# Source order on three engines in a Strassen-Winograd up-projection, rotating staging places and respaced norm steps

## The chip, the cores and the metric

The kernel runs on one core of a Trainium2 chip. The metric is device time of one execution in microseconds. Engines: PE is TensorE (matmul; PEld its weight loads), DVE is VectorE, ACT is ScalarE, POOL is GpSimd, SP is SyncE, which only issues DMAs here.

## The reference

One inference step of a two-layer decoder trunk with width 1024: 1024 prompt tokens and eight decode tokens, which the kernel carries as 1032 columns. Layer 1 is an HGRN2 recurrence, layer 2 a sliding-window attention, each beside a cross-attention into 256 memory tokens. Both end in an output projection and a squared-ReLU MLP of width 4096:

```python
mix = jnp.concatenate([tok_out, x_out], axis=-1) @ w_out[l]
h = h + rms_norm(mix, norm_post_mix[l])
u = jnp.square(jax.nn.relu(rms_norm(h, norm_pre_mlp[l]) @ w_up[l]))
h = h + rms_norm(u @ w_down[l], norm_post_mlp[l])
```

Outputs are the hidden states, the memory keys and values, the recurrent state and the last 128 keys and values.

## The kernel before

Everything is f32. A product is made of three matmuls (`mm3`, lines 287 to 289): operands are split into a high part (a cast on ScalarE, line 225) and a low part (a subtraction on GpSimd, line 98), and low x high, high x low and high x high are summed in PSUM. VectorE's instructions all pass through the wrapper `InOrder` and therefore show as line 51.

`mlp` is run once per layer. Its up-projection has 32 output tiles of 128 rows. Six are plain dense tiles. The other 26 are taken as 13 pairs, and `pair` computes a pair by the seven block products of a Strassen-Winograd scheme, which the code names 11, 22, S2, 12, S3, S1 and S4. Each product is 24 matmuls of 128x258 (two column halves c = 0 and 1, four blocks, three matmuls), so a pair is 168 matmuls. Products accumulate into PSUM banks: 11 and 12 into `ac` (two banks), 22 and S1, S4 into `ax` (four), S2 and then S3 into the same two `dn` banks. So S3 can't start in a half before VectorE has added that half's S2 result into `u2` (the rows `k<-k,dn`).

For the next pair, `load_blocks` has ScalarE issue four weight DMAs (`wr<-wu`), `sum_blocks` forms S1 to S4 of the weights on VectorE (four operations of 128x512), and `split_block` splits the seven blocks one by one into a ring of ten places (ScalarE cast, GpSimd subtraction).

A pair's last part, `last()`, is put behind the next pair's first product (`pending`): it splits the hidden block B21 into the tile `mv` (`split_21`) and stores it with one DMA (`u21s<-mv`), runs product S4, forms three hidden differences on VectorE and one on GpSimd (`hidden_sums`, 128x516), and then takes one item off the list `late`. That list has 12 items for the first six plain tiles' hidden blocks: `load` (four DMAs `ct<-u` on ScalarE's queue) and `rest` (split of that B21 into the same `mv`, and the hidden differences of 128x258 on `ct` tiles), alternating, so a `load` in one pair and its `rest` in the next. The tag `mv` has one buffer, `ct` six.

A scheduler (the TileContext) orders each engine's instructions by its own planned times, not by the source. Only an instruction that is passed to `tc.keep_in_program_order` keeps source order on its engine; before, these are VectorE's, and only in a part of the down-projection (`ordered[0]`).

Norms are cut into small steps that wait on a list `bg`; `tick(n)` runs n of them on average between the matmul groups of another stage. `post_norm` puts there: statistics of the residual branch (`stat`), their broadcast (`stat_b`, a matmul at line 197), eight steps, the statistics of the next norm (`stat_next`, matmuls of 86x1 at line 177) and their use. `out_late` is the end of the first layer's output projection (three column chunks of 344, eight output tiles each); `out_b` is the second layer's.

Of the kernel before, what the change touches and what calls it, by code (L numbers as in the profile page):

```python
# [34 lines left out]
def trunk_kernel(ctx, tc, xT, memT, wia, wib, wkk, wkv, wmk, wo, wu, wd, cmk, cmv, sth, ssk, ssv,  # L35
                 gains, sinkb, sinkc, cosd, sind, identd, lvmd, swmd,
                 yT, mko, mvo, hpo, kpo, vpo, hso, kso, vso):
    nc = tc.nc
    ordered = [False]

    class InOrder:


        def __init__(self, eng):
            self.eng = eng

        def __getattr__(self, name):
            f = getattr(self.eng, name)

            def call(*args, **kw):  # L50
                r = f(*args, **kw)  # L51
                return tc.keep_in_program_order(r) if ordered[0] else r
            return call

    V, A, T, G, S = nc.vector, nc.scalar, nc.tensor, nc.gpsimd, nc.sync
    V = InOrder(V)
    uid = [0]

    def nm(s):
# [814 lines left out]
    u2 = const([RB, N // RB], "u2")  # L874
    u4 = const([RB, N // RB], "u4")

    def post_norm(Y, a, w, acc, gpost, hsrc, hdst, nxt, scaled, bank="ac", rbank="ax", direct=False):

        hts, box = [], {}
        per = N // w
        sl, bl = slice(a, a + w), slice(a // RB, (a + w) // RB)

        def row(k):
            return hts[k // per][:, k % per]

        def stat():
            for i, k0 in enumerate(range(0, KT, per)):  # L890
                ht = slot("p" if i < 2 else "t", (P, per, w))
                n = min(per, KT - k0)
                for src, o in rows(hsrc, k0, n, a, w):
                    S.dma_start(ht[:, :n, o], src)
                hts.append(ht)
            st = rstd_tok(acc, square=u4[:, bl] if scaled else None, bank=rbank)
            if scaled:
                tt(V, st, st, u2[:, bl], ALU.mult)
            box["r"] = spread(st)

        def stat_b():
            box["r"] = bcast(box["r"], bank)

        def step(k):
            y, h = Y[k][:, sl], row(k)
            V.scalar_tensor_tensor(y, y, gain(gpost, k), box["r"], op0=ALU.mult, op1=ALU.mult)
            tt(V if k % 4 == 3 else G, y, y, h, ALU.add)
            for dst, o in rows(hdst, k, 1, a, w):
                S.dma_start(dst, y[:, o].unsqueeze(1))
            if nxt is None:  # L910
                return
            A.activation(h, y, AF.Square)
            if k % 4 and not direct:
                r = row(k - k % 4)
                tt(V if k < 4 else G, r, r, h, ALU.add)
            hi, lo = X[:, k, 0, sl], X[:, k, 1, sl]
            if scaled:
                split(y, hi, lo, G if k % 4 == 1 else V)
            else:
                split_gain(y, gain(nxt, k), hi, lo)  # L920

        def stat_next():
            if nxt is None:
                return
            st = rstd_tok(*(row(k) for k in range(0, KT, 1 if direct else 4)), bank=rbank)
            if scaled:
                box["n"] = spread(st)
            else:
                tt(V, u2[:, bl], st, st, ALU.mult)
                tt(V, u4[:, bl], u2[:, bl], u2[:, bl], ALU.mult)  # L930

        def next_b():
            if nxt is not None and scaled:
                A.copy(nxt[:, sl], bcast(box["n"], bank))
        bg.extend([stat, stat_b] + [lambda k=k: step(k) for k in range(KT)] + [stat_next, next_b])

    Y_TAGS = ["q", "k", "q", "k", "k", "k", "k", "k"]

# [33 lines left out]
    def out_late(l, box, ws, hsrc, hdst):  # L972
        Y = box["Y"]
        accs = slot("t", (P, NCH, CH))
        Y += [slot(t) for t in ("q", "q", "k", "k")]

        def full(m, c):
            def ev(c, ps):
                A.copy(Y[m][:, cs(c)], ps)
                sumsq(accs[:, c], Y[m][:, cs(c)], m == ME, G if m % 2 else V)  # L980
            dense_chunk(ws[1 + m - ME], c, ev, ks=EARLY + LATE)

        def rest(m, c):
            ps = dense_bank()[:, :CH]
            w = ws[0]
            for i, k in enumerate(LATE):
                o = m * 256 + i * P
                mm3(ps, w[0][:, o:o + P], w[1][:, o:o + P], X[:, k, 0, cs(c)], X[:, k, 1, cs(c)], i == 0, i == 1)
            y = Y[m][:, cs(c)]
            tt(V, y, y, ps, ALU.add)  # L990
            sumsq(accs[:, c], y, False, V if m % 2 else G)

        wide[0] = True
        for c in range(NCH):
            for m in (4, 5, 6, 7, 0, 1, 2, 3):
                (full if m >= ME else rest)(m, c)
                tick()
            post_norm(Y, c * CH, CH, accs[:, c], G_POSTMIX + 8 * l, hsrc, hdst, G_PREMLP + 8 * l, False)
        return Y

# [48 lines left out]
    def mlp(l, hsrc, hdst, nxt, Yp):  # L1049
# [42 lines left out]
        def plain_sums(j, c):  # L1092

            ps = []

            def load():
                ps.extend(chunk_tile(CW) for _ in range(4))
                for n, p in zip(("11", "12", "21", "22"), ps):
                    A.dma_start(p, ub[n][j][:, c * CW:(c + 1) * CW])

            def rest():
                split_21(j, c * CW, ps[2])
                hidden_sums(j, c * CW, *ps)
            return [load, rest]

# [174 lines left out]
        sum_blocks()  # L1280
        for n in us:
            split_block(us, n)
        for i in range(NPAIR):
            nxt_us = names(i + 1) if i + 1 < NPAIR else None
            pair(i, us, nxt_us)
            us = nxt_us
        for f in pending:
            f()


        Y = [slot(t) for t in Y_TAGS]
# [152 lines left out]
            weight_load(n)  # L1444
        for n in range(SPLIT, len(ust)):
            hidden_load(n)
        ordered[0] = True
        for n in range(SPLIT):
            hidden_split(n)
            weight_split(n)  # L1450
# [2 lines left out]
        for n, (p, cc, (g, m)) in enumerate(units):  # L1453
            if n + LOAD < len(units):
                weight_load(n + LOAD)
            if n + STAGE < len(units):
                hidden_load(n + STAGE)
            if n + SPLIT < len(units):
                hidden_split(n + SPLIT)
            if n + SPLIT < len(units):  # L1460
                weight_split(n + SPLIT)
            w = split_at.pop(n)
            for c in cc:
                if g == 0:
                    banks[m, c] = bank(p, m, c)
                t = slice(E2[c], E2[c + 1]) if p == 2 else slice(c * CW, c * CW + CW)
                second = p == 2 and c == 0 and m % 2 == 1
                for j in range(4):
                    k, o = 4 * (n // 4 % 2) + j, slice(j * P, j * P + P)
                    mm3(banks[m, c], w[:, 0, o], w[:, 1, o], X[:, k, 0, t], X[:, k, 1, t],  # L1470
                        g == 0 and j == 0 and not second, g == 3 and j == 3, p == 2)
                if g == 3:
                    evac(p, m, c, banks[m, c])
            if p == 3 and g == 1:
                for c in range(2):
                    squares(1, 1, m, c, G)
            if p == 4 and g == 1:
                squares(0, 0, m, cc[0], G)
            if (g, m) == (3, 3):
                if p == 3:  # L1480
                    bg.append(lambda: None)
                    norm(1, 1)
                    norm(1, 0)
                if p == 4:
                    if cc[0] == 0:
                        bg.extend([lambda: None] * 2)
                    norm(0, cc[0])
            elif p in (2, 4):
                tick(1.6 if p == 2 else 1)
            if n + SPLIT >= half:  # L1490
                ordered[0] = False


    def swa_values(wv, vt, kvn, c, r1):
# [356 lines left out]

    for n, c in enumerate((2, 1, 0)):
        if n == 1:
            cq_chunk(1, 2)
        dense_chunk(w0, c, ev0)
        if n == 0:
            tick(1)
            V.tensor_copy(rn, R2[:, NP_:])
            cq_chunk(0, c)
            tick(3)  # L1860
        if n == 1:
            tick(len(bg))
            load_late(f32(mv), mvd)
            for i in range(2):
                load_late(f32(k2[i]), k2d[i])
            tt(V, cosb, cosb, R2, ALU.mult)
            tt(G, sinb, sinb, R2, ALU.mult)
        if n == 2:
            keys[0]()
        rstd_cols(R2, c, r8, r1)  # L1870
        if n:
            for p in range(2):
                cq_chunk(p, c)
        swa_values(wv, vt, kvn, c, r1)
# [52 lines left out]
    for c in range(NCH):  # L1927
        for m in (*range(3, KT), *range(3)):
            if c or m > 4:
                (full if m > 3 or c == 2 else rest)(m, c)  # L1930
                tick()
        norm(c)
    mlp(1, hs[2], yT, None, [YB[m] for m in range(KT)])
    tick(len(bg))
# [102 lines left out]
```

## Time and profile before

| | |
|---|---|
| median of three runs | 2537.7 us (2537.47 to 2540.87) |
| the profiled execution | 2528.82 us |
| its span | 2526.9 us, mean granted clock 0.971 |
| PE busy | 2337.0 us (92%) |
| DVE, ACT, POOL busy | 1693.0, 1105.7, 1423.9 us |
| pair loop of layer 1 | about 726 to 1011 us from the span's start |
| pair loop of layer 2 | about 1878 to 2163 us |
| end of the first output projection | about 577 to 655 us |

Times in the trace are microseconds from the span's start. The granted clock is given as a share of 2.4 GHz, so 0.50 is 1.2 GHz. "A <- B" reads: A waited for B. A DMA that an engine issues stands in that engine's queue (ACTq, SPq) among its other instructions.

### The profile page before, as it was taken

How to read it: one execution, taken by the hardware profiler on the slowest of the kernel's cores; microseconds unless marked ns; L12 is line 12 of the kernel's file. 1: busy time of each engine (PE TensorE's matmuls, PEld its weight loads, DVE VectorE, ACT ScalarE, POOL GpSimd, SP SyncE). 2: the span in 40 equal slices, each digit the busy share in tenths (PEclk: the TensorE clock that was granted, in tenths of full speed). 3: DMA queues.
4: the chain of work that ended last, by engine and by line, in shares of the span. 5: the costliest groups of instructions: out<-in, count | busy, mean ns of one | idle time of the engine just before them, and what ended most of it. 6: DMA issues, size and time to landing. Idle time of an engine off the chain costs nothing. (4 is left out here: it accounts for less than half of the span.)

```text
span 2526.9 us, 45370 instructions
## 1 busy us (share of the span) xinstructions
PE 2337.0 (92%) x17055; PEld 2258.4 (89%) x17055; DVE 1693.0 (67%) x2813; ACT 1105.7 (44%) x2457; POOL 1423.9 (56%) x1130
## 2 busy tenths in 40 slices
PE   7998999989899999999999998888999999999997
PEld 6887989989799989999998897777999899999996
DVE  7778677775766665677667367765576665667847
ACT  6573434444433232444354364664443333344424
POOL 4546454453676564657775344544576556557846
PEclk9999999999999999999999998999999999999998
DMA  4335555432345555755663333333335545855482
GB/s 160 134 109 177 164 179 168 161 95 84 113 138 165 167 183 175 246 162 149 197 214 112 106 105 97 108 111 132 120 113 167 171 156 171 277 148 152 127 279 74
DMA packets 231735, 383.00 MB, mean 152 GB/s; under 512 B 27914, under 2 KB 118602, under 8 KB 231500
## 3 DMA queue, kind: packets, MB, share of 16 engines
q1 hardware_dynamic: 154332, 253.80, 30.1%
q10 hardware_dynamic: 77184, 126.31, 17.1%
q8 instruction: 134, 2.20, 0.4%
q14 instruction: 85, 0.70, 0.1%
HBM read 253.27 MB, written 123.56 MB: 149 GB/s over the span
## 5 line engine op out<-in xcount | busy, mean ns | idle before, releaser
L287 PE MATMUL dn<-X,ws 128*128 128x344 f32 (+2 forms) x1136 | 374.0, 330 | 30.8 <-DVE X L51 17.7
L288 PE MATMUL dn<-X,ws 128*128 128x344 f32 (+2 forms) x1136 | 369.0, 325 | 0.0
L289 PE MATMUL dn<-X,ws 128*128 128x344 f32 (+2 forms) x1136 | 368.2, 324 | 0.0
L98 POOL TENSOR_TENSOR ws<-wr,ws 128x512 fp32r<-128x512 f32 (+1 forms) x118 | 222.4, 1887 | 172.3 <-ACT ws L225 161.9
L287 PEld LDWEIGHTS dn<-X,ws 128*128 128x128 f32 x1136 | 219.2, 193 | 41.7 <-DVE X L51 20.2
L51 DVE TENSOR_TENSOR X<-ws,X 128x516 fp32r<-128x516 f32 x160 | 179.6, 1127 | 107.0 <-ACT X L225 106.4
L288 PEld LDWEIGHTS dn<-X,ws 128*128 128x128 f32 x1136 | 219.6, 193 | 1.9 <-issue 0.8
L289 PEld LDWEIGHTS dn<-X,ws 128*128 128x128 f32 x1136 | 219.4, 193 | 1.2 <-issue 0.4
L288 PE MATMUL ax<-X 128*128 128x258 f32 x736 | 209.5, 285 | 2.2 <-POOL X L98 2.2
L287 PE MATMUL ax<-X 128*128 128x258 f32 x736 | 207.8, 284 | 3.0 <-ACT X L225 3.0
L289 PE MATMUL ax<-X 128*128 128x258 f32 x736 | 209.1, 285 | 0.0
L225 ACT CAST ws<-wr 128x1024 fp32r<-128x1024 f32 (+1 forms) x138 | 116.1, 843 | 148.1 <-DMA wfd<-ws 35.5
L98 POOL TENSOR_TENSOR p<-p,sm 128x512 f32<-128x512 f32 (+2 forms) x92 | 87.5, 974 | 127.3 <-DVE sm L51 66.7
L225 ACT CAST X<-ws 128x516 fp32r<-128x516 f32 (+1 forms) x192 | 110.1, 621 | 101.1 <-PE ax L289 48.3
L287 PE MATMUL ax<-X,ws 128*128 128x344 f32 (+2 forms) x472 | 148.0, 315 | 3.1 <-DVE X L51 2.7
L289 PE MATMUL ax<-X,ws 128*128 128x344 f32 (+2 forms) x472 | 145.8, 309 | 0.0
L288 PE MATMUL ax<-X,ws 128*128 128x344 f32 (+2 forms) x472 | 145.5, 308 | 0.0
L287 PE MATMUL ac<-X 128*128 128x258 f32 x496 | 140.2, 284 | 4.6 <-ACT k L1231 3.8
L288 PEld LDWEIGHTS ax<-X 128*128 128x128 f32 x736 | 140.8, 191 | 2.6 <-POOL X L98 2.6
L287 PEld LDWEIGHTS ax<-X 128*128 128x128 f32 x736 | 140.0, 191 | 3.4 <-ACT X L225 3.4
L289 PE MATMUL ac<-X 128*128 128x258 f32 x496 | 140.5, 284 | 0.0
L289 PEld LDWEIGHTS ax<-X 128*128 128x128 f32 x736 | 140.5, 191 | 0.0
(650 smaller groups left out, 8198.3 us busy)
## 6 DMA issues: line engine op xcount, KB each, us to landing
ws<-u ACTq DMA_DIRECT2D x160, 258.0 KB, 2.8
u<-k SPq DMA_DIRECT2D x104, 258.0 KB, 3.9
wr<-wu ACTq DMA_DIRECT2D x104, 256.0 KB, 3.1
wfd<-ws SPq DMA_DIRECT2D x20, 1024.0 KB, 5.0
X<-u21s SPq DMA_DIRECT2D x32, 516.0 KB, 6.3
ct<-u ACTq DMA_DIRECT2D x112, 129.0 KB, 2.7
u<-k SPq DMA_DIRECT2D x104, 129.0 KB, 1.8
u21s<-mv SPq DMA_DIRECT2D x26, 516.0 KB, 3.8
```

Of the source, the lines that this page charges most:

```text
L51: r = f(*args, **kw)
L98: return eng.tensor_tensor(out, a, b, op=op)
L225: A.copy(hi, src)
L287: T.matmul(ps, wh, xl, start=first, stop=False, skip_group_check=more)
L288: T.matmul(ps, wl, xh, start=False, stop=False, skip_group_check=more)
L289: T.matmul(ps, wh, xh, start=False, stop=last, skip_group_check=more)
```

## The change

It has six parts. (1) `InOrder` wraps ScalarE and GpSimd too, and in the loop over the 13 pairs all three keep source order; TensorE and the DMA queue of SP don't. In the down-projection VectorE alone is kept, as before. Every wrapped instruction now shows as line 51. (2) A plain tile's B21 is split into two of the six rotating `ct` places instead of `mv`, and stored by two DMAs. (3) `post_norm` has empty steps between its statistics, broadcasts and the eight steps. (4) `out_late` takes its output tiles in the order 4, 0, 5, 1, ... and ticks 2 after each instead of 1.5. (5) Ticks in the down-projection are 2.2 and 1.1 instead of 1.6 and 1, and two empty steps are gone. (6) In the shared K/V stage the list is run down to `AFTER` steps before one chunk, a tick is 2 instead of 1, and `out_b` ticks 2.

```diff
@@ the wrappers @@
-    ordered = [False]
+    ordered = set()

     class InOrder:
-        def __init__(self, eng):
-            self.eng = eng
-
-        def __getattr__(self, name):
-            f = getattr(self.eng, name)
+        def __init__(self, eng, name):
+            self.eng, self.name = eng, name
+
+        def __getattr__(self, attr):
+            f = getattr(self.eng, attr)

             def call(*args, **kw):
                 r = f(*args, **kw)
-                return tc.keep_in_program_order(r) if ordered[0] else r
+                return tc.keep_in_program_order(r) if self.name in ordered else r
             return call

-    V, A, T, G, S = nc.vector, nc.scalar, nc.tensor, nc.gpsimd, nc.sync
-    V = InOrder(V)
+    T, S = nc.tensor, nc.sync
+    V, A, G = InOrder(nc.vector, "V"), InOrder(nc.scalar, "A"), InOrder(nc.gpsimd, "G")
@@ post_norm @@
-        bg.extend([stat, stat_b] + [lambda k=k: step(k) for k in range(KT)] + [stat_next, next_b])
+        gap = [lambda: None]
+        bg.extend([stat] + gap + [stat_b] + [lambda k=k: step(k) for k in range(KT)] + 2 * gap + [stat_next] + gap
+                  + [next_b])
@@ out_late @@
-            for m in (4, 5, 6, 7, 0, 1, 2, 3):
+            for m in (4, 0, 5, 1, 6, 2, 7, 3):
                 (full if m >= ME else rest)(m, c)
-                tick()
+                tick(2)
@@ plain_sums @@
             def rest():
-                split_21(j, c * CW, ps[2])
+                hi, lo = (slot("ct", (P, CH), F32R)[:, :CW] for _ in range(2))
+                split(ps[2], hi, lo, G)
+                for i, t in enumerate((hi, lo)):
+                    S.dma_start(u21[i, j][:, c * CW:(c + 1) * CW], f32(t))
                 hidden_sums(j, c * CW, *ps)
@@ mlp, around the pair loop @@
+        ordered.update("VAG")
         for i in range(NPAIR):
...
         for f in pending:
             f()
+
+        ordered.clear()
@@ mlp, down-projection @@
-        ordered[0] = True
+        ordered.add("V")
...
                 if p == 4:
-                    if cc[0] == 0:
-                        bg.extend([lambda: None] * 2)
                     norm(0, cc[0])
             elif p in (2, 4):
-                tick(1.6 if p == 2 else 1)
+                tick(2.2 if p == 2 else 1.1)
             if n + SPLIT >= half:
-                ordered[0] = False
+                ordered.clear()
@@ shared K/V stage @@
         if n == 1:
+            tick(len(bg) - AFTER)
             cq_chunk(1, 2)
         dense_chunk(w0, c, ev0)
         if n == 0:
-            tick(1)
+            tick(2)
@@ out_b @@
                 (full if m > 3 or c == 2 else rest)(m, c)
-                tick()
+                tick(2)
```

On VectorE, in the pair where the second plain item is finished (names: `k` are room for hidden pieces, `wr` and `q` the weight blocks, `ct` plain-tile pieces, `dn` and `ax` PSUM banks; the numbers are buffers), before:

```order
L51 TENSOR_TENSOR k_6780<-k_6781,k_6780 128x516
L51 TENSOR_TENSOR k_6781<-k_6781,k_6782 128x516
L51 TENSOR_TENSOR k_6783<-k_6782,dn_8091 128x258
L51 TENSOR_TENSOR ct_8788<-ct_8790,ct_8788 128x258
L51 TENSOR_TENSOR k_6783<-k_6782,dn_8092 128x258
L51 TENSOR_TENSOR ct_8790<-ct_8790,ct_8787 128x258
L51 TENSOR_TENSOR k_6778<-wr_6777,wr_6776 128x512
L51 TENSOR_TENSOR k_6778<-k_6778,wr_6776 128x512
L51 TENSOR_TENSOR wr_6777<-wr_6776,wr_6777 128x512
L51 TENSOR_TENSOR ct_9279<-ct_9280,ct_9279 128x258
```

And the same place of a later plain item after the change:

```order
L51 TENSOR_TENSOR k_6780<-k_6781,k_6780 128x516
L51 TENSOR_TENSOR k_6781<-k_6781,k_6782 128x516
L51 TENSOR_TENSOR ct_8793<-ct_8794,ct_8793 128x258
L51 TENSOR_TENSOR ct_8794<-ct_8796,ct_8794 128x258
L51 TENSOR_TENSOR ct_8796<-ct_8796,ct_8793 128x258
L51 TENSOR_TENSOR k_6778<-wr_6777,wr_6776 128x512
L51 TENSOR_TENSOR k_6778<-k_6778,wr_6776 128x512
L51 TENSOR_TENSOR wr_6777<-wr_6776,wr_6777 128x512
L51 TENSOR_TENSOR q_6779<-wr_6777,k_6778 128x512
L51 TENSOR_TENSOR k_6783<-k_6782,dn_9083 128x258
L51 TENSOR_TENSOR k_6783<-k_6782,dn_9084 128x258
```

The three differences of `ct` stood between the two evacuations of `dn` and behind the weight sums; now they stand together, ahead of the weight sums and of both evacuations.

On ScalarE, around the loads of a plain item (`mv` and `ct` casts are B21's high parts), before:

```order
L1157 DMA wr_6776<-wu 128x512
L225 CAST mv_7555<-ct_7313 128x258
L1157 DMA wr_6777<-wu 128x512
L225 CAST X<-k_6778 128x512
L1099 DMA ct_8297<-u_0_6045 128x258
L225 CAST X<-wr_6777 128x512
L1099 DMA ct_8298<-u_0_6046 128x258
L225 CAST X<-k_6778 128x512
L1157 DMA wr_6777<-wu 128x512
L1099 DMA ct_8787<-u_0_6044 128x258
L1247 ACTIVATE k_6784<-ac_7483 128x258
L1099 DMA ct_8788<-u_0_6051 128x258
```

After, the loads of an item in one pair:

```order
L51 COPY k_6780<-ac_7733 128x258
L51 COPY k_6780<-ac_7734 128x258
L51 CAST mv_7765<-k_6784 128x516
L51 DMA ct_7805<-u_0_6044 128x258
L51 DMA ct_7806<-u_0_6051 128x258
L51 DMA ct_7807<-u_0_6045 128x258
L51 DMA ct_7808<-u_0_6046 128x258
L51 CAST ws_6773<-wr_6776 128x512
L51 CAST ws_6774<-wr_6776 128x512
```

and the first casts of the next pair, in which the item is used:

```order
L51 COPY k_6782<-ac_7977 128x258
L51 COPY k_6782<-ac_7978 128x258
L51 CAST mv_8009<-k_6781 128x516
L51 CAST ct_8049<-ct_7807 128x258
L51 CAST X<-wr_6776 128x512 x2
```

The four loads from `u` stood one by one between casts and weight loads, two of them behind the cast into `mv` whose item they belong to; now they stand together, ahead of that pair's casts, and the cast of the plain B21 goes into `ct`, one pair later.

## Rows read from the trace of the kernel before

**Rows 1.** Page, busy us (share of the span) and instructions of each engine.

```profile
PE 2337.0 (92%) x17055; PEld 2258.4 (89%) x17055; DVE 1693.0 (67%) x2813; ACT 1105.7 (44%) x2457; POOL 1423.9 (56%) x1130
```

**Rows 2.** Windows: start:end, us, busy us (x instructions) per engine, clock, DMA.

```profile
726.00:1011.00 285.00, 267.43 (x2148) 265.77 (x2148) 177.50 (x302) 85.76 (x182) 164.95 (x124) 0.96 0.55 173
1878.00:2163.00 285.00, 266.04 (x2129) 264.05 (x2129) 173.75 (x299) 85.54 (x182) 164.60 (x124) 0.96 0.54 171
1050.00:1100.00 50.00, 50.00 (x420) 50.00 (x419) 31.39 (x36) 23.45 (x45) 26.00 (x17) 1.00 0.46 129
```

**Rows 3.** TensorE's waits, 726 to 1011: us in total, times, longest.

```profile
PE dn L287 <- DVE k L51: 12.0, 4, 3.8
...
PE ac L287 <- ACT k L1231: 2.5, 1, 2.5
```

**Rows 4.** Windows of ten half-clock stretches, their sum, and another.

```profile
854.00:860.80 6.80, 5.38 (x25) 5.38 (x26) 4.77 (x10) 2.41 (x6) 2.30 (x2) 0.50 0.40 120
...
2099.80:2103.20 3.40, 3.40 (x18) 3.40 (x17) 3.37 (x8) 0.62 (x1) 0.49 (x1) 0.50 0.49 160
sum 40.80, PE 37.88 PEld 37.79 DVE 29.47 ACT 16.62 POOL 13.95; mean PE 3.79 PEld 3.78 DVE 2.95 ACT 1.66 POOL 1.39
...
900.20:906.00 5.80, 5.80 (x48) 5.80 (x49) 4.20 (x8) 2.42 (x6) 2.67 (x2) 1.00 0.52 154
```

**Rows 5.** Waits of all engines, 750 to 995.

```profile
DVE ct L51 <- DMA ct<-u: 33.2, 7, 8.2
...
ACT mv L225 <- DMA wr<-wu: 19.1, 5, 4.4
```

**Rows 6.** Timeline of VectorE: start, us, instruction xcount, [idle before <-releaser].

```profile
846.01 0.42 DVE L51 TENSOR_TENSOR k<-k,dn 128x258 f32<-128x258 f32 x1
854.61 0.43 DVE L51 TENSOR_TENSOR ct<-ct,ct 128x258 f32<-128x258 f32 x1 [8.18 <-DMA ct<-u]
854.95 0.42 DVE L51 TENSOR_TENSOR k<-k,dn 128x258 f32<-128x258 f32 x1
```

**Rows 7.** Timeline of ScalarE and its DMA queue, same stretch.

```profile
843.89 0.41 ACT L225 CAST mv<-ct 128x258 fp32r<-128x258 f32 x1 [3.70 <-DMA u21s<-mv]
...
855.74 0.35 ACTq L1099 DMA_DIRECT2D ct<-u  x1
```

**Rows 8.** Timeline of TensorE, same stretch.

```profile
855.42 0.58 PE L287 MATMUL dn<-t,ws 128*128 128x258 f32 x1 [3.75 <-DVE k L51]
```

**Rows 9.** Timeline of TensorE at 900.

```profile
900.14 0.39 PE L287 MATMUL dn<-t,X 128*128 128x258 f32 x1 [1.78 <-DVE k L51]
```

**Rows 10.** VectorE's groups, 750 to 995: xcount, busy us, mean ns, idle before.

```profile
L51 DVE SCALAR_TENSOR_TENSOR k<-k 128x258 f32<-128x258 f32 x70 | 42.9, 625 | 1.3
L51 DVE TENSOR_TENSOR k<-k,k 128x516 f32<-128x516 f32 x28 | 28.7, 1023 | 1.6
L51 DVE TENSOR_TENSOR k<-k,ax 128x258 f32<-128x258 f32 x70 | 28.2, 414 | 14.2 <-PE ax L289 13.9
L51 DVE TENSOR_TENSOR q<-wr,k 128x512 f32<-128x512 f32 x11 | 12.9, 1175 | 0.0
L51 DVE TENSOR_TENSOR k<-k,wr 128x512 f32<-128x512 f32 x11 | 10.3, 934 | 0.3
L51 DVE TENSOR_TENSOR k<-wr,wr 128x512 f32<-128x512 f32 x10 | 9.5, 950 | 21.2 <-DMA wr<-wu 10.6 <-DMA u<-k 8.6 <-POOL ws L98 2.0
L51 DVE TENSOR_TENSOR wr<-wr,wr 128x512 f32<-128x512 f32 x11 | 7.5, 681 | 0.0
L51 DVE TENSOR_TENSOR ct<-ct,ct 128x258 f32<-128x258 f32 x11 | 6.4, 583 | 33.2 <-DMA ct<-u 33.2
```

**Rows 11.** TensorE's waits from 610 to 655, and one window of it.

```profile
PE ax L177 <- DVE p L51: 5.9, 2, 3.9
PE dn L287 <- DVE k L51: 5.3, 1, 5.3
...
640.00:650.00 10.00, 1.64 (x5) 1.28 (x6) 10.00 (x12) 5.60 (x14) 8.00 (x7) 0.62 0.67 234
```

More of the change, by code (lines that the diff above doesn't have):

```diff
@@ L875, in trunk_kernel @@
     u4 = const([RB, N // RB], "u4")
+    AFTER = 5
     def post_norm(Y, a, w, acc, gpost, hsrc, hdst, nxt, scaled, bank="ac", rbank="ax", direct=False):
```

## Prediction

> **What bounds the kernel now.** I began with the busy line of the page: TensorE works 2337.0 us of a span of 2526.9, the other three at most 1693.0 [rows 1]. So only TensorE's idle time, 190 us in all, and the time that its clock is held down can be won. Next came the windows by stage. In the down-projection TensorE is busy for 50.00 of 50.00 us at clock 1.00, with 420 matmuls of 258 columns [rows 2], so one such matmul takes 50.00 / 420 = 0.119 us and a pair (168 of them) 20.0 us. The two pair loops, 726 to 1011 and 1878 to 2163, should look the same and don't: TensorE is idle for 285.00 - 267.43 = 17.6 us and 285.00 - 266.04 = 19.0 us there, at clock 0.96 [rows 2]. The clock loss I read from ten stretches at 0.50 (1.2 GHz instead of 2.4), five in each loop: TensorE is busy 37.88 us in them, and half of that, 18.9 us, is the price of the lower level [rows 4]. The loops together lose 17.6 + 19.0 + 18.9 = 55.5 us. That is the prize of this change.
>
> Who is late? In the first loop TensorE waits 12.0 us, four times, for VectorE to empty a dn bank, and once 2.5 us at the loop's start for a ScalarE copy [rows 3]. A clock stretch follows the longer stalls: after the 3.75 us that end at 855.42 there are 6.8 us at 0.50, while after the 1.78 us that end at 900.14 the clock stays 1.00 [rows 4, 8, 9].
>
> Why VectorE is late stands in the waits of all engines: it stands still 33.2 us, seven times, for loads of ct from u [rows 5]. One instance, instruction by instruction: VectorE evacuates the first dn half at 846.01, then meets a ct difference whose operand hasn't landed and idles 8.18 us, and only behind that comes the evacuation of the second half at 854.95, for which TensorE stands till 855.42 [rows 6, 8]. The load is late because of ScalarE, which issues it: the cast into mv at 843.89 had stood 3.70 us behind the transfer that reads the single mv buffer, with the loads behind it in the queue; at 855.74 one is only being issued [rows 7]. So each stall is a head-of-line wait: a product that TensorE needs stands behind a plain tile's difference that nobody needs yet. It returns every second pair, where the plain items' second half runs.
>
> **The change part by part.** *Source order on ScalarE and GpSimd, and two rotating places for a plain B21.* In the new order ScalarE issues the four ct loads of a plain tile back to back, and the differences on VectorE come one pair later (20.0 us), before the weight sums; the new cast goes into a ct place and so has no wait on u21s<-mv. At the slowest, seven such waits cost 33.2 us, 4.7 each, so 20 us of lead covers them four times. I cost this wait at 0. VectorE's instructions are the same in kind and number, ScalarE's and GpSimd's too; one DMA becomes two of half the bytes on SP's queue, 12 issues more, behind which only stores stand: 0.
>
> What is late next is VectorE's own chain, which is now rigid: from the end of the first half of product S4 to the evacuation that frees the first dn half for product S3. Worked from [rows 10]: the second half of S4 ends 12 matmuls later (1.43), add and square 0.414 + 0.625; three hidden differences of 516, 3 x 1.023; four weight sums 0.950 + 0.934 + 0.681 + 1.175; the evacuation 0.42. Sum 9.7 us, and with three ct differences of 0.583 in every second pair 11.4 us. Against it I count in the new order of TensorE's instructions 88 to 91 matmuls between the same two points (101 in the first two of the pairs that carry ct differences), that is 10.5 to 10.8 us. TensorE's order is new as well: between S2's last matmul and S3's first stand 36 to 60 others, from the fifth pair on 58 to 60, where it was 24 in every pair. So pairs without ct differences stall 0, and the four of six with them 11.4 - 10.8 = 0.6 to 0.7 us, too short for the clock by the 1.78 us row. Four times 0.7 is 2.8 us a loop. The loop's start keeps one stall of 2.5 us (the same ScalarE copy, behind the same casts) and its clock stretch, 3.40 / 2 = 1.7 us. Left: 2.8 + 2.5 + 1.7 = 7.0 us a loop, 14 in both. **Gain 55.5 - 14 = 41.5 us.**
>
> Bounds of the chain. Least: the three differences and four sums all at the mean of the cheapest sum, 0.681: 1.43 + 1.04 + 7 x 0.681 + 0.42 = 7.7 us. Most: all seven at the dearest sum's 1.175, and square and ct differences dearer by the ratio of the two, 1.7: 1.43 + 0.41 + 1.06 + 8.23 + 0.42 = 11.6 us, with ct differences (3 x 0.99) 14.5. I take the means, since they hold the mixture that GpSimd's splits beside them cause now, and GpSimd has the same work in the same 20 us.
>
> The last point has a rule of its own. In the trace, four weight sums of one shape and one kind average from 0.681 to 1.175 us by what runs beside them [rows 10]. The Trainium skill, "SBUF — State Buffer", section "Who interferes with whom", says that a VectorE instruction with two SBUF inputs contends with a GpSimd instruction that reads SBUF, and that whichever issues first holds the shared port for its whole length while the other is fully blocked. The spread agrees with it. By that rule a new order can line each of these sums up behind a split; by the means of the rows the sum below is 2499 us, by that rule at its worst rival 2's 2572.
>
> *Norms in the first layer's output projection.* Between 577 and 655 TensorE waits 5.9 us in two pieces (2.0 and 3.9) for the operands of the next norm's statistics and 5.3 us for a dn bank; VectorE is busy 10.00 of the 10.00 us from 640, TensorE 1.64 at clock 0.62 [rows 11]. Fillers don't make VectorE faster here. By the order the statistics matmul of the first chunk now comes 63 matmuls behind the broadcast instead of 85, that of the second 61 instead of 43. These matmuls are 344 wide, so 0.119 x 344 / 258 = 0.159 us: 22 fewer is 3.5 us less cover in the first chunk, 18 more is 2.9 us more in the second. With some clock lost to a longer first stall I take **+3 us**, between -5 (the dn stall gone) and +8 (first stall 2.0 + 3.5 with its clock stretch, none won in the second).
>
> *Ticks* in the down-projection, the shared K/V stage and the second layer's output projection move norm steps by a few matmuls; the matmuls around the waits there stand nearly where they did. 0, give or take 4 us; below zero as well as above, since the planner orders the rest anew.
>
> Sum: 2528.8 (span 2526.9 and 1.9 around it) - 41.5 + 3 = 2490.3 us on the scale of the profiled execution. The median of the runs is 2537.7, so 8.9 above that execution; **forecast 2490.3 + 8.9 = 2499 us**.
>
> **The rivals.** *1. VectorE's chain becomes a bound in every pair.* For: the slack is small, 10.5 against 9.7 us. If the chain grows by 1.5 us, 24 pairs stall 0.6 and 8 of them 2.2: 24 x 0.6 + 8 x 1.6 = 27 us, with the two starts (8.4) 36 and some clock 4. Gain 55.5 - 40 = 15; with +3 this is 2526 us. *2. Slower: the contention of VectorE and GpSimd.* In source order the weight sums stand beside the splits of the preceding blocks in each pair. At the upper end, 11.6 and 14.5 us, 24 pairs stall 1.1 or 3.7, 2.4 in the mean, and half of them with 1.7 of clock: 24 x 2.4 + 12 x 1.7 = 78 us, with the starts 86, against 55.5 now: 2537.7 + 31 + 3 = 2572 us. It decides from a mean stall of (55.5 - 8.4 - 3) / 24 = 1.8 us a pair, a chain of 12.4 us. Against: no row has all of the chain's operations at their dearest together. *3. The change doesn't do what it says.* ct loads still land late, since ScalarE in strict order stands on a wait for a weight load or for a PSUM bank, and the loads behind it. For: even now ScalarE's casts into mv come 19.1 us late, five times, with wr<-wu named last [rows 5]. Against: a full pair lies between load and use. The stalls stay at 55.5: 2537.7 + 3 = 2541, within 0.2% (5 us, about what a measurement of this kernel can tell from no change), or a little faster.
>
> **How the numbers follow.** Forecast 0.67, rival 1 0.16, rival 3 0.09, rival 2 0.08. The forecast's own range: the starts gone too and the norms at -5 is 2537.7 - 55.5 - 5 - 4 = 2473 at the most; I take 2484, a residue of 7 us and the norms at 0, to 2516 where the norms take 8, the ticks 4 and the chain 5. The range goes to 2532 to take in rival 1. Faster by over 0.2%: 0.67 + 0.15 and a little of rival 3, 0.82. Within 0.2%: 0.09. Slower: 0.09.
>
> **What would show it.** Right: in both loops TensorE's idle time falls from 17.6 and 19.0 us to under 8, the clock reads 0.99, VectorE's wait for ct<-u is gone from the waits, and no cast waits for u21s. Wrong in the chain: TensorE waits for VectorE's k before dn in nearly every pair, 0.5 to 2 us. Wrong in the bounds: the 512 wide sums average over 1.2 us. Wrong in the norms: the wait for p in the first output projection outside 0 to 8 us for its first piece. A stall at the loop's start over 3 us, or a stage outside the loops that moves by more than 5 us, would also break the sum.

## The result and the profile after

| | before | after |
|---|---|---|
| median (six runs each) | 2539.28 us (2533.95 to 2542.77) | 2551.96 us (2550.25 to 2560.02) |
| ratio of the times, 95% interval | | 1.0053 (1.0036 to 1.0070) |
| the profiled execution's span | 2526.9 us | 2558.2 us |

The change made the kernel 0.5% slower; the forecast (2499 us) was 1.6% faster. The two profiled executions lie further apart than the medians: that of before (2528.82 us) is below all six runs of the table, that of after the slowest of its six. So places are compared below and not the sums of the two traces. Of the runs further below, one of `e3_loop_parts_released` took 4471.78 us; that kernel's time and ratio are those of its other four.

Where the time went shows when the moments are compared at which TensorE has issued the same number of its 17055 matmuls. The table is worked out from the start times of the matmuls in the two traces; it gives the length of each stretch before, and how much longer it is after (a pair is 168 matmuls).

| matmuls | stretch | before, us | after, us |
|---|---|---|---|
| 3100 to 3900 | first output projection | 136.6 | +7.3 |
| 4230 to 6000 | pair loop of layer 1, its first ten and a half pairs | 240.0 | -14.8 |
| 6000 to 6620 | rest of the loop, start of the down-projection | 76.2 | +20.7 |
| 12200 to 13900 | pair loop of layer 2, its first ten pairs | 233.5 | -19.5 |
| 13900 to 14480 | rest of the loop, start of the down-projection | 71.3 | +21.4 |

What lies ahead of these stretches, between them and behind them is 16 us longer after. How much such a comparison can tell is seen where a stage was left alone: in the eleven runs below whose first output projection is that of before, its stretch is between 0.5 us shorter and 4.1 us longer, and two executions of one kernel (e9 and e15) differ there by 2.4 us.

**The loops gained most of what was forecast.** The windows over the pair loops (start:end, us, busy us of the engines, granted clock, DMA share, GB/s), which answer to [rows 2]:

```profile
740.00:1012.00 272.00, 260.30 (x2124) 256.89 (x2122) 199.66 (x300) 83.39 (x182) 172.03 (x123) 0.99 0.53 180
1905.00:2176.00 271.00, 260.86 (x2141) 257.43 (x2141) 201.00 (x304) 83.98 (x183) 172.85 (x124) 1.00 0.54 183
```

They take 272 and 271 us instead of 285, with 24 matmuls fewer (some 3 us) in the first and 12 more in the second, and the clock is 0.99 and 1.00 instead of 0.96. TensorE's idle time falls from 17.6 and 19.0 us to 11.7 and 10.1; under 8 was forecast. With the one half-clock stretch that is left (3.4 us, so 1.7) the loops lose 23.5 us instead of 55.5: a gain of 32, where 41.5 was forecast. TensorE's waits in the first loop (us in total, times, longest), which answer to [rows 3]:

```profile
PE dn L287 <- DVE k L51: 7.5, 11, 1.9
PE ax L287 <- DVE k L51: 2.1, 1, 2.1
PE ac L287 <- ACT k L51: 2.1, 3, 0.7
```

For dn there were four waits of 12.0 us in sum; now there are eleven, of 0.7 us in the mean. The longest, 1.88 us in the first pair, is followed by the half-clock stretch; behind the others the clock stays 1.00. VectorE's 33.2 us of waiting for ct<-u [rows 5] have gone from the list.

**The place that was not forecast is the seam behind each loop.** First TensorE's longest wait from 1005 to 1045 and from 2140 to 2215, then VectorE's timeline at the first seam, then the window of its half-clock stretch:

```profile
PE dn L287 <- DVE X L51: 15.3, 1, 15.3
PE dn L287 <- DVE X L51: 16.5, 1, 16.5
```

```profile
1016.33 1.43 DVE L51 TENSOR_TENSOR k<-k,k 128x516 f32<-128x516 f32 x2
1024.69 1.47 DVE L51 TENSOR_TENSOR k<-k,k 128x516 f32<-128x516 f32 x1 [6.93 <-DMA u<-k]
1026.08 3.77 DVE L51 TENSOR_TENSOR ct<-ct,ct 128x258 f32<-128x258 f32 x3
1029.77 4.25 DVE L51 TENSOR_TENSOR X<-ws,X 128x516 fp32r<-128x516 f32 x6
```

```profile
1017.70:1034.80 17.10, 4.20 (x20) 4.23 (x20) 9.25 (x11) 4.21 (x8) 11.13 (x9) 0.50 1.05 360
```

TensorE waits for an X, that is for the low part of the down-projection's first hidden block. VectorE makes it at 1029.77, behind leftovers of the last pair: a hidden difference that overwrites a piece whose store hasn't been read yet (6.93 us of waiting), and the three differences of the last plain item. The clock falls to 0.50 inside the wait, at 1017.70, and stays there for 17.1 us; TensorE is busy for only 4.20 of them, so the lower level costs some 2 us. The second seam is the same, with 16.5 us. The order of VectorE's instructions at this place says it already; before:

```
L51 TENSOR_TENSOR k_6781<-k_6781,ax_9889 128x258
L51 TENSOR_TENSOR X<-ws_9998,X 128x516
L51 SCALAR_TENSOR_TENSOR k_6781<-k_6781 128x258
L51 TENSOR_TENSOR X<-ws_9998,X 128x516
```

and after:

```
L51 TENSOR_TENSOR k_6781<-k_6781,k_6782 128x516
L51 TENSOR_TENSOR ct_9777<-ct_9778,ct_9777 128x258
L51 TENSOR_TENSOR ct_9778<-ct_9780,ct_9778 128x258
L51 TENSOR_TENSOR ct_9780<-ct_9780,ct_9777 128x258
L51 TENSOR_TENSOR X<-ws_10010,X 128x516 x3
```

Before, only the down-projection's VectorE instructions were kept in order, and the planner laid the pair's leftovers between them. Now leftovers and down-projection are one chain in source order.

**The first output projection.** TensorE's waits from 575 to 665 after the change, which answer to [rows 11]:

```profile
PE ax L177 <- issue: 11.0, 1, 11.0
PE ax L177 <- DVE p L51: 5.1, 1, 5.1
```

The first wait for the statistics grew from 2.0 to 5.1 us, the second place from 3.9 plus the dn wait of 5.3 to 11.0. Sum 16.1 instead of 11.2.

### The profile page after: what moved, and what is told of

The parts are those of the page before. It is cut to its first block, busy times and chain, and to the rows that moved or that the text cites. A ratio compares the mean times of both kernels' runs of the same rounds, so it can differ in the third digit from the quotient of the medians.

```text
span 2558.2 us, 45314 instructions
## 1 busy us (share of the span) xinstructions
PE 2342.6 (92%) x17055; PEld 2260.7 (88%) x17055; DVE 1744.3 (68%) x2813; ACT 1099.9 (43%) x2457; POOL 1437.9 (56%) x1130
## 3 DMA queue, kind: packets, MB, share of 16 engines
q10 hardware_dynamic: 77184, 126.31, 16.2%
## 4 chain that ended last, share of the span: by engine, by line
PE 53%; DVE 21%; DMA 10%; issue 7%; ACT 6%; POOL 3%; SPq 1%; ACTq 0%; DVEq 0%; POOLq 0%
PE dn L287 8%; PE dn L288 7%; PE dn L289 7%; PE ax L288 6%; PE ax L287 6%; PE ax L289 6%; DVE k L51 6%; DVE q L51 4%; DVE X L51 2%; DVE p L51 2%; PE ac L288 2%; PE ac L289 2%; PE ac L287 2%; DVE r L51 2%; DMA X<-u21s 2%
## 5 line engine op out<-in xcount | busy, mean ns | idle before, releaser
L51 DVE TENSOR_TENSOR X<-ws,X 128x516 fp32r<-128x516 f32 x160 | 167.5, 1058 | 121.0 <-ACT X L51 121.0
L287 PEld LDWEIGHTS dn<-X,ws 128*128 128x128 f32 x1136 | 221.7, 195 | 31.0 <-DVE X L51 15.9
L288 PEld LDWEIGHTS dn<-X,ws 128*128 128x128 f32 x1136 | 222.8, 196 | 1.9 <-issue 0.8
L289 PEld LDWEIGHTS dn<-X,ws 128*128 128x128 f32 x1136 | 222.9, 196 | 1.2 <-issue 0.4
L287 PEld LDWEIGHTS ax<-X 128*128 128x128 f32 x736 | 139.7, 190 | 7.3 <-DVE k L51 3.8
L288 PEld LDWEIGHTS ax<-X 128*128 128x128 f32 x736 | 140.0, 190 | 2.6 <-POOL X L51 2.6
L287 PE MATMUL ac<-X 128*128 128x258 f32 x496 | 140.0, 284 | 1.4 <-ACT k L51 1.4
L288 PE MATMUL ac<-X 128*128 128x258 f32 x496 | 140.4, 284 | 0.0
L289 PE MATMUL ac<-X 128*128 128x258 f32 x496 | 140.2, 283 | 0.0
```

What stands on the lines that cost most here:

```text
L287: T.matmul(ps, wh, xl, start=first, stop=False, skip_group_check=more)
L288: T.matmul(ps, wl, xh, start=False, stop=False, skip_group_check=more)
L289: T.matmul(ps, wh, xh, start=False, stop=last, skip_group_check=more)
```

## The experiments

The theory after the result: the loops gain, the seam takes it back, and the norm steps cost a little. Ratios are to the kernel before, on the same chip, with 95% intervals; kernels from different chips are compared by their ratios.

**Is the seam the order's?** In `e1_release_before_last` the changed kernel's order ends ahead of the leftover work:

```diff
-        for f in pending:
-            f()
-
         ordered.clear()
+        for f in pending:
+            f()
```

> The changed kernel with one edit: source order ends before the last pair's leftover work (its product S4, differences and the last plain item) instead of behind it. Theory A (the order on VectorE that runs on from the loop into the down-projection makes the first splits of the down-projection stand behind the last plain item, 15.3 and 16.5 us of TensorE idle at 1030 and 2194 and the clock stretch of 17.1 us behind each): both stalls fall under 3 us, the time falls by about 40 us to 2512 (2502 to 2520). Theory B (the stall is the transfers': the stores and loads at the end of the loop are late whatever the order): stalls over 10 us stay, 2545 to 2555.

Measured 2531.5 us, 0.9957 (0.9944 to 0.9969): 0.96% or 24 us below the changed kernel (1.0053), where about 40 were expected. The waits of TensorE from 1005 to 1045 in it, first two rows:

```profile
PE ac L287 <- DVE X L51: 3.3, 1, 3.3
PE dn L287 <- DVE X L51: 1.1, 1, 1.1
```

The long stall is gone, so theory B falls. What was not expected is that the stretch of matmuls 6000 to 6620 is still 8.6 us longer than before (10.1 at the second seam): nearly half of the stretch's price is something else.

**The loop's parts alone, with the seam and without.** `e2_loop_parts` is the changed kernel with parts 3 to 6 taken back; `e3_loop_parts_released` is that with the edit of e1.

> The kernel before with the loop's two parts alone: source order on three engines in the pair loop, and the plain B21 in rotating ct places; norm steps, output order and ticks as before. Theory A (the loops gain about 35 us in TensorE's waits and clock, the two seams give 42 back, the norm parts cost the rest): about 2541 (2533 to 2549), no change against before, with both seam stalls of over 12 us. Theory B (the norm steps and ticks are what costs): about 2505, as the loop's gain would come through.

> As e2_loop_parts, and source order ends before the last pair's leftover work. Theory A: 2541 - 40 = 2501 (2493 to 2510), with TensorE idle under 10 us in each loop and no stall over 3 us at the seams. Theory B (the seam isn't the order's): 2541 as e2_loop_parts. If the norm parts are worth something instead of costing, it lies above e1_release_before_last; theory A wants it about 10 us below.

e2 took 2544.4 us, 1.0010 (0.9998 to 1.0021), no difference to before. e3 took 2522.4, 0.9920 (0.9906 to 0.9934). Between them lie 0.90% or 23 us, about as between the changed kernel and e1 (0.96%). The loops gain 17.3 and 19.4 us in e2, 15.8 and 19.4 in e3 (the same stretches as in the table); the seams take 20.6 and 21.9 in e2, 12.4 and 8.5 in e3.

**The norm parts alone.** `e4_norm_parts` is the kernel before with parts 3 to 6.

> The kernel before with parts 3 to 6 alone: spaced norm steps, the order and ticks of the output projections, ticks of the down-projection and the K/V stage; the loop as before. Theory A: about 10 us slower than before, 2549 (2543 to 2556), with the wait of the second chunk's statistics in the first output projection near 11 us instead of 9.2 in two pieces, and the first one's near 5 instead of 2. Rival (these parts pay for themselves, and the rest of the loss is in the loop's edit): 2530 to 2539.

2556.2 us, 1.0045 (1.0032 to 1.0058). The waits stand where they were expected:

```profile
PE ax L177 <- issue: 11.0, 1, 11.0
PE ax L177 <- DVE p L51: 5.2, 1, 5.2
```

The first output projection is 5.2 us longer than before. The rest of the 11 us (0.45% of 2540) has two places in the trace. One is at the end of the second layer's down-projection (matmuls 16400 to 16700): it is 3.7 us longer, with a wait of TensorE for VectorE's q of 3.2 us instead of 1.4 and a half-clock stretch. The changed kernel and e1, which have the same parts, are 3.7 and 4.4 us longer there, with the same wait of 3.3 and 3.2; in the other kernels this place differs from before by 1.0 us at most. The other is the pair loop, which e4 has as before: its first ten pairs are 6.3 us longer in layer 1 and 4.9 in layer 2, with more waiting for dn (17.0 us instead of 12.0 in layer 1).

**Which of the norm parts?** `e8_first_projection` is parts 3 and 4 alone, `e12_tile_order_alone` part 4 alone (tile order and ticks, no empty steps).

> The kernel before with parts 3 and 4 alone: the spaced norm steps and the first output projection's tile order and ticks. e4_norm_parts with all of parts 3 to 6 is 14 us over the kernel before. Theory A (the early statistics matmul in the first output projection is the larger part): 2548 (2545 to 2553). Rival (the loss is in the ticks of the later stages, parts 5 and 6): 2540 to 2544.

> The kernel before with part 4 alone: the first output projection's tiles in the order 4, 0, 5, 1, ... and ticks of 2, without the empty norm steps. In e4 the two waits for the next norm's statistics there are 5.2 and 11.0 us, where before they are 1.9, 5.3 (a dn bank) and 3.9. Theory A (the earlier ticks bring the statistics matmul ahead of its operands): the waits grow here too, to 15 us or more in sum, 2546 (2543 to 2550). Theory B (the empty steps do it): 11 us as before or less, 2540 (2536 to 2543).

e8 took 2554.5 us, 1.0052 (1.0034 to 1.0070). It computes other hidden states than before in the second layer (presumably a step there reads an operand before it is renewed, with the longer list of steps and the old later ticks; no run shows which), so only its first layer can be set beside the others: 7.1 us more in the first output projection. e12 took 2548.5 us, 1.0040 (1.0022 to 1.0057). Its waits from 575 to 665:

```profile
PE ax L177 <- issue: 12.6, 1, 12.6
PE ax L177 <- DVE p L51: 5.2, 1, 5.2
```

So tile order and ticks alone bring the long wait, 17.8 us instead of 11.2; the empty steps neither make it nor mend it (16.2 in e4). And part 4 alone has most of the price of all four norm parts (0.40% of 0.45%). Some of it stands in the unordered pair loop of layer 1: its first ten pairs are 7.1 us longer in e12, 6.1 in e8 and 6.3 in e4, and 1.2 us shorter in e11 below, which has the same loop without part 4. Why the unordered loop waits more behind the new tile order was not asked. In the ordered loop the norm parts make no such difference: it is 2.5 us longer in the changed kernel than in e2 and 1.0 shorter in e1 than in e3.

**The seam alone.** `e11_seam_alone` is the kernel before with VectorE kept in order over the leftover work only, without any gain in the loop.

```diff
+        ordered[0] = True
         for f in pending:
             f()
+        ordered[0] = False
```

> The kernel before with VectorE in source order over the last pair's leftover work alone, so that this order and the down-projection's join, and nothing else: the disputed cost by itself, without the loop's gain. Theory A (the seam costs what the trace of the changed kernel shows there, 18.7 us at each of two seams): 2540 + 37 = 2577 (2565 to 2585), with a stall of 12 us or more ahead of the down-projection. Theory B (a seam stall arises only because the reordered loop ends in another state): 2540 (2535 to 2546).

2559.8 us, 1.0084 (1.0061 to 1.0108): 20.5 us slower by nothing but the joined order. (The 18.7 us a seam that theory A took stand in no row; by the table it is 20.7 and 21.4.) TensorE waits at the two seams:

```profile
PE dn L287 <- DVE X L51: 13.5, 1, 13.5
```

```profile
PE dn L287 <- DVE X L51: 12.8, 1, 12.8
```

The stretches at the seams are 14.3 and 13.9 us longer than before. The mechanism is shown; the size is little more than half of what was expected, and within the intervals it is what releasing the order gives back (24 us in e1, 23 in e3).

**What in the loop brings the gain?** In `e6_order_without_places` e3 has its plain B21 back in the single mv buffer. `e7_vector_only` is e3 with VectorE alone in order, `e9_vector_order_alone` the kernel before with VectorE's order and nothing else:

```diff
+        ordered[0] = True
         for i in range(NPAIR):
...
+        ordered[0] = False
         for f in pending:
             f()
```

> As e3_loop_parts_released, with the plain B21 split back in the single mv buffer and stored by one DMA. Theory A (source order alone brings the ct loads forward; the wait for the mv buffer now stalls only ScalarE, which has the time): within 6 us of e3, 2524 (2519 to 2530). Theory B (the mv wait is the root: 3.7 to 4.2 us of ScalarE in each pair with a plain item, behind which ScalarE's relus of product 12 and the next casts stand): 2535 to 2545.

> As e3_loop_parts_released, with source order on VectorE alone in the loop; ScalarE and GpSimd are left to the planner. Theory A (the gain comes from ScalarE issuing the ct loads a pair ahead; VectorE in order with late loads has the whole chain behind them): slower than e3 by 10 or more, 2535 to 2560. Theory B (what counts is VectorE's order, ScalarE's and GpSimd's is idle detail): 2524 (2518 to 2529).

> The kernel before with a single edit: VectorE alone keeps source order in the pair loop, released ahead of the last pair's leftover work; the plain B21 stays in the single mv buffer. Theory A (VectorE's order is the whole of the loop's gain; the planner, knowing it, has the ct loads issued early by itself, and the mv wait costs ScalarE nothing that counts): 2517 (2511 to 2523), no wait for ct<-u over 1 us on VectorE. Theory B (either ScalarE's source order or the rotating places are needed, as the e6 and e7 kernels each kept one of them): 2530 or more, with waits for ct<-u of several us back.

e6: 2516.5 us, 0.9904 (0.9886 to 0.9921). e7: 2517.6, 0.9908 (0.9891 to 0.9926). e9: 2522.3, 0.9934 (0.9912 to 0.9957), and run again as `e15_vector_order_again` 2523.2, 0.9919 (0.9902 to 0.9936).

> The kernel of e9_vector_order_alone again, for comparison on the same chip: 2522 (2517 to 2526), 0.993 of the time of before.

None of the three differs from e3 by more than the intervals allow, so ScalarE's and GpSimd's order and the rotating places are worth nothing that shows. Theory A of e7 falls, and so does theory B of e6 and of e9. The waits in e9 from 725 to 1000 make it plain:

```profile
ACT mv L225 <- DMA u21s<-mv: 29.8, 5, 7.1
DVE ct L51 <- DMA ct<-u: 8.6, 2, 5.2
```

The wait for the mv buffer is still there, 29.8 us (before, 18.8 from 750 to 995, and 19.1 more of these casts put down to weight loads [rows 5]), and so it is in e6 (28.9). ScalarE has the time. What fell is VectorE's wait, from 33.2 to 8.6 us, though not as far as expected: two waits of 5.2 and 3.5 us are left, where none over 1 us was expected. The differences now keep their place one pair behind the loads. In e9 the loads of an item are issued at 852.49 to 855.43 and its first difference starts at 887.17; before, loads issued at 846.53 and 849.23 were waited for till 854.61. In e7 the loop is tightest of all; TensorE's waits there from 725 to 1000:

```profile
PE dn L287 <- DVE k L51: 3.4, 8, 1.2
PE ac L287 <- ACT k L51: 2.9, 1, 2.9
```

**What still binds the seam?** `e5_last_pair_free` (e3) and `e10_vector_order_last_free` (e9) leave the last pair to the planner as well.

> As e3_loop_parts_released, and the last of the 13 pairs is left to the planner as well. In e3 the last product ends 7 us earlier than before, but the down-projection's first operands land as late as before (TensorE idle 5.4 us at 1009.72), and some 10 us a layer are given back there. Theory A (the planner needs the last pair's room to bring the hidden blocks' loads forward): the stall at the seam falls under 2 us, 2523.6 - 10 = 2513 (2508 to 2518). Theory B (the hidden blocks can't be loaded before the last products are stored, so the seam is bound by transfers): 2523 (2519 to 2527).

> As e9_vector_order_alone, with the last of the 13 pairs left to the planner too. By e5 against e3 (2519 against 2524): 3 to 5 us below e9, 2513 (2508 to 2519). If the seam is bound by the hidden blocks' loads whatever the order, the same as e9 within 2 us.

e5: 2518.8 us, 0.9912 (0.9886 to 0.9938), against 0.9920 of e3. e10: 2520.8, 0.9926 (0.9908 to 0.9944), against 0.9934 of e9. Neither difference shows, the seams stay 8 to 11 us longer than before, and the stall that theory A wanted under 2 us is 4.8 in e5. The windows of ten us at the seam, of the kernel before and of e3, have another candidate (columns as above; the last three are clock, DMA share, GB/s):

```profile
990.00:1000.00 10.00, 10.00 (x86) 10.00 (x85) 5.15 (x11) 1.38 (x3) 1.39 (x1) 1.00 0.32 118
1000.00:1010.00 10.00, 10.00 (x85) 10.00 (x84) 2.93 (x7) 2.54 (x6) 2.51 (x2) 1.00 1.01 310
1010.00:1020.00 10.00, 9.26 (x77) 9.05 (x76) 9.10 (x15) 5.16 (x9) 4.92 (x4) 1.00 1.00 351
```

```profile
990.00:1000.00 10.00, 10.00 (x86) 10.00 (x85) 6.95 (x13) 0.41 (x1) 3.61 (x4) 1.00 0.97 277
1000.00:1010.00 10.00, 4.61 (x37) 4.40 (x37) 3.20 (x8) 4.11 (x10) 2.70 (x2) 0.98 1.02 289
1010.00:1020.00 10.00, 10.00 (x73) 10.00 (x74) 7.61 (x13) 5.02 (x9) 5.05 (x4) 0.85 1.00 327
```

The DMA engines are full from 1000 on before, and from 990 in e3: the down-projection's first operands and the last stores are under way. In e3 TensorE has finished the loop's last product at 1004 instead of 1011 and then stands for 5.4 us, till 1009.72; before, the first product of the down-projection starts at 1011.43. So most of what the last pair wins is lost at once. The stall has the clock behind it too: 0.85 in the ten us from 1010, where before it reads 1.00. Over matmuls 6000 to 6620 TensorE is idle for 9.9 us in e3 (1.3 before) and busy at half clock for 6.7, which costs 3.3; these two make up 11.9 of the 12.4 us. Why the operands come no earlier is the question that is left. Two kernels asked whether it is the amount of transfers: both are e9 with six copies of 258 KB that nobody reads, at the end of the loop or in its middle.

> As e9_vector_order_alone, with six copies of 258 KB in memory added in the last pair of each loop, 1.55 MB, whose results nobody reads. Theory A (the seam is bound by the DMA engines, which are full there and move 284 to 372 GB/s): 1.55 MB at 0.34 MB a us is 4.6 us later at each seam, some 9 us over e9, 2531 (2527 to 2537). Theory B (order or latency binds, not the amount): as e9, 2522 (2518 to 2526).

> As e13_transfers_at_seam, with the same copies in the seventh pair, where the DMA share is about 0.55: the control. Both theories: as e9, 2522 (2518 to 2526). If it is as slow as e13, the copies cost through the store queue in which they stand and not through the full DMA engines.

e13: 2528.0 us, 0.9936 (0.9911 to 0.9960). e14: 2526.5, 0.9939 (0.9919 to 0.9960). The times don't tell them apart. In the traces the two seams are 12.3 and 12.7 us longer than before in e13, 10.3 and 9.9 in e14, 9.7 and 8.1 in e15: 2 to 5 us for the copies at the seam, where theory A wanted 4.6, but each from one execution, and the copies were issued from 959 on, ahead of the full stretch. This stays open.

## Why the prediction was wrong, by its own steps

- **The step that failed is "What is late next".** It followed the chain to the next product of the same loop and ended there. The last round of the loop has another successor, the down-projection, whose VectorE instructions were already in source order: two ordered stretches that meet become one. The term for the seam was 0 ("a stage outside the loops that moves by more than 5 us" was only named as a way to fail). The trace of the changed kernel has +20.7 and +21.4 us there; the joined order alone costs 24 us by the changed kernel against e1, and 20.5 in e11.
- **The gain was also counted to the loop's end.** What the loop wins is not handed on in full: with the order released the seams still take 7 to 12 us each (e3, e6, e7, e9), so a loop's 14 to 23 us are worth some 3 to 15. The whole of a released order is 17 to 24 us (0.9934 in e9 to 0.9904 in e6), not 41.5. Why the seam keeps this much stays open.
- **What bounds the kernel, and why VectorE is late:** right in the symptom. The head-of-line wait behind a ct difference was the loops' loss. The root, "the load is late because of ScalarE", was wrong as a cure: with ScalarE's mv wait still there, VectorE's order alone takes most of the wait away (e9).
- **"I cost this wait at 0":** right, no wait of VectorE for ct<-u is left in the changed kernel. (4.7 us is the mean of the seven waits and not the slowest, which is 8.2 [rows 5]; a lead of 20 us covers that as well.)
- **VectorE's chain, 9.7 and 11.4 us against 10.5 to 10.8:** right in kind, and too small. In the first loop the five pairs with ct differences stall 0.7 to 1.0 us, where 0 was forecast for two of them and 0.6 to 0.7 for the others; the first pair stalls 1.9 and the others up to 0.5, where 0 was forecast. Idle time and clock leave 13.4 and 10.1 us in the loops instead of 7.0 each. The three hidden differences were cheaper than the means used (0.697 instead of 1.023 us). The weight sums were dearer: they average 1.40 us, so the sign "512 wide sums over 1.2 us" came, and three of the four lie over the 1.175 that was taken as the dearest (the last section has their rows).
- **"Too short for the clock by the 1.78 us row":** the row doesn't carry that. In e3 a wait of 1.73 us was followed by 3.4 us at half clock (last section).
- **Norms, +3 us between -5 and +8:** the first output projection was 5.2 us longer in e4, 7.3 after, of which up to 4 come and go in kernels that leave this place alone: inside the bounds. The first wait was forecast at 2.0 + 3.5 = 5.5 and measured 5.1. The second was to shrink by 2.9 and grew; that the dn wait moves into it was not seen. "Ticks, 0 give or take 4": 3.7 to 4.4 us at the end of the second layer's down-projection, in each of the three kernels that have parts 5 and 6 and in no other. Norm parts and ticks together cost 9 us (e1 against e3, 0.37%) where +3 was forecast.
- **Rival 2** priced contention over 1.8 us a pair: it came, but the stalls average under 1.0. **Rival 1** came in part, as short stalls. **Rival 3** was not it: no ct load was late.
- **Two sums of the range are off:** with a residue of 7 us and the norms at 0 its lower end is 2537.7 - 48.5 = 2489 and not 2484, and 2516 counts the norms' 8 us on top of the 3 that are in 2499 already. Both are small beside the miss.

The miss of 52 us (38.5 faster forecast, 13 slower measured) splits by the ratios of e3, e1 and the changed kernel, which add one group of parts at a time: loop parts with the order released -20 us instead of -41.5, norm parts and ticks +9 instead of +3, the joined order at the seam +24 instead of 0. Three edits of the kernel before that have no part in common add up to about the same total: e9 (-0.66%), e11 (+0.84%) and e4 (+0.45%) give +0.63%, against +0.53% (0.36 to 0.70) measured. In part that is luck, since some of e4's loss stands in the unordered loop, which the changed kernel doesn't have.

## What to carry to other kernels

Where an order is fixed for a stretch, look at both of its ends: what stands behind the stretch's last instructions on that engine, and whether that was free to pass them before. A leftover that hides well inside a loop (a difference for later use, a wait for a store) becomes the head of the line for the next stage. And fix as few engines as do the job: here VectorE's order alone, ended ahead of the leftover work, gives 0.992 to 0.993 of the time of before (e9 and e15).

## What the runs showed of the hardware

Four operations of one shape on one engine come at very different prices. VectorE's groups in the changed kernel from 750 to 995 (xcount, busy us, mean ns of one, idle before), which answer to [rows 10]:

```profile
L51 DVE TENSOR_TENSOR q<-wr,k 128x512 f32<-128x512 f32 x12 | 20.2, 1686 | 0.0
L51 DVE TENSOR_TENSOR k<-k,k 128x516 f32<-128x516 f32 x28 | 19.5, 697 | 1.9 <-DMA u<-k 0.3
L51 DVE TENSOR_TENSOR wr<-wr,wr 128x512 f32<-128x512 f32 x11 | 19.5, 1773 | 0.0
L51 DVE TENSOR_TENSOR k<-k,wr 128x512 f32<-128x512 f32 x11 | 15.6, 1420 | 0.4
L51 DVE TENSOR_TENSOR k<-wr,wr 128x512 f32<-128x512 f32 x11 | 7.5, 682 | 0.0
```

In a fixed order each weight sum has its fixed company. The first (`k<-wr,wr`) starts while GpSimd is idle and takes 0.682 us. Each of the others starts some 0.5 us into a GpSimd operation and ends 0.55 us behind the end of that operation, in all 33 cases that start in this window: the second (`k<-k,wr`) beside GpSimd's hidden difference, at 1.12 or 1.67 us, the third and fourth beside its splits, at 1.75 to 1.79. The splits pay too: 1.71 to 1.75 us there, and 1.30 where VectorE stands idle (at 1006.91). The Trainium skill, "SBUF — State Buffer", section "Who interferes with whom", has such VectorE instructions contend with GpSimd instructions that read SBUF; the trace agrees, and the price is up to 1.1 us for an instruction of 0.68.

The length of one wait doesn't decide what the clock does. It went to 0.50 for 3.4 us behind a wait of 1.88 us that ended at 750.82 in the changed kernel, and behind one of 1.73 us that ended at 745.47 in e3, while before a wait of 1.78 us that ended at 900.14 left it at 1.00 [rows 4, 9]. TensorE had been busy for 7.12 of the 9 us up to 751.00, for 7.27 of the 9 up to 746.70 and for 7.22 of the 9 up to 900.20.
